# Two thirds of the modulation's product on ScalarE and GpSimd, in a two-block network on one Trainium2 core

## The chip, the cores and the metric

The kernel runs on one core of a Trainium2 chip. The engines are TensorE (PE in the profile; PEld is its weight load), VectorE (DVE), ScalarE (ACT), GpSimd (POOL) and SyncE (SP, which issues most of the DMAs). The metric is the device time of one execution in microseconds. A change below about 0.5% can't be told from none.

## The reference

The input is x, 256 tokens of 1024 channels, in fp32. Two blocks follow each other. The first has mixers and a feed-forward, and a norm at its end:

```python
x = x + concat([y_sc, y_gdn, y_sb]) @ w_mix_out
h = rmsnorm(x, w_norm_ffn)
u = causal_dwconv(h @ w_ffn_up, w_ffn_conv)      # 1024 -> 2 * 2816, 3 taps
gate, val = split(u)
x = x + (silu(gate) * val) @ w_ffn_down
```

The second block is modulated by a vector c of 1024 numbers. Six vectors of 1024 are made of it by one vector-matrix product and used in the norms and the residuals; two kinds of attention and a mixture of 32 experts, of which each token takes 4, are the block's layers:

```python
mod = silu(c) @ w_ada + b_ada                    # 1024 -> 6 * 1024
sh1, sc1, gt1, sh2, sc2, gt2 = split(mod, 6)
h = rms_norm(x, g_pre_mix) * (1 + sc1) + sh1
x = x + gt1 * rms_norm(attention(h) @ w_out, g_post_mix)
h2 = rms_norm(x, g_pre_ffn) * (1 + sc2) + sh2
x = x + gt2 * rms_norm(moe_ffn(h2), g_post_ffn)
```

## The kernel before

The program is one straight sequence: block 1's mixers (0 to 183 us), its feed-forward (183 to 396), the norms between the blocks (396 to 405), block 2's attention (405 to 545), the router, and the experts (565 to the end).

**Weights.** The dense weights and the modulation's come in one stream of slabs, 128x2048 fp32, 1 MB each, in the order `WS`, through the six places of pool A (`NA`). `load_slabs` issues on SyncE's queue the load of slab n once slab n - 6 is read. `ADA_AT` says before which dense slab each of the 24 modulation slabs stands; four (`WX`) are not in the stream but have places of their own in pool `fx`, loaded in turns 2 to 5 of the feed-forward. After the stream pool A takes six of the experts' slabs.

**Units and splits.** Half a dense slab is a unit of weights, 128x1024. A product in full fp32 is made of three fast ones, so each unit is split into a high and a low part (`split`): ScalarE copies the high 12 bits (L388), VectorE subtracts them (L393; in a few places GpSimd does), both into one of four places of pool C, tile `u`. `split_ahead` writes the splits up to four units ahead of the products, so the split of unit u + 4 waits until the products of unit u are done.

**The feed-forward.** Its loop runs 11 turns. In a turn i, `up(2 * i)` and `up(2 * i + 1)` take two units each, 24 products a unit (L433) into a PSUM bank; ScalarE takes the bank out with the first tap (L1040, `fcv`), VectorE adds the two others from the bank (L1043). The gate gets its SiLU on ScalarE (L1048), VectorE multiplies (L1049), and the product is split too: `gh` on ScalarE (L1052), `gl` on VectorE (L1053). From turn 1 on, two `down` units follow (12 products each, lines L467 to L469). The four last `down` units come behind the loop, in `last_products`, the first 128 tokens' products before the others', so that the norm of the first half (`add_norms`) runs beside the products of the second.

**The modulation.** `ada(i)` makes 16 of the 48 chunks of 128 from 8 slabs. [...] All 8 slabs add up in one PSUM bank. Then ScalarE copies the bank (`adar`, L489), four transposes turn it (L493), and VectorE adds the bias into `mod` (L494). `ada(0)` runs in the mixers and at the feed-forward's start. Of `ada(1)`, four slabs run at the end of the turns 7 to 10, three after the first half of the norms and one after the second (L483); of `ada(2)`, all eight run in the attention, two after each of the first four heads' keys, in the generator `projections2`. `shifts` makes from the modulation the router's biases and the residual's scales.

**Order.** Everything is written out by hand; in the mixers and the attention `weave` picks between chains by estimated times. Each engine does its instructions in the order in which they were written. `keep_warm(n)` (L292) writes n products that nobody reads, at seven places, with the counts of `WARM`.

Of the kernel before, what the change touches and what calls it, by code (L numbers as in the profile page):

```python
# [10 lines left out]
F32 = mybir.dt.float32  # L11
# [22 lines left out]
# The pools that hold the experts' first slabs; those of pool O hold only one.  # L34
# [4 lines left out]
F1 = 3  # L39
LAST = 2  # L40
# Products that keep the tensor engine's clock up, by place.
WARM = (4, 6, 9, 1, 2, 9, 12)

# Slots of the experts by rank: the first two are experts 0 and 1, the others come by falling count of tokens.
# [4 lines left out]
# The stream of dense weights: ("s", i), slabs of the products; ("a", i), slabs of the modulation, put before the slab  # L49
# of the products with the number given.  # L50
N_DENSE = 67
ADA_AT = [14] * 3 + [20] * 5 + [38, 41, 44, 47] + [-1] * 4 + [54] * 2 + [55] * 2 + [56] * 2 + [57] * 2
# [3 lines left out]
# Slabs of the modulation that have places of their own.  # L56
WX = [("a", j) for j in range(24) if ADA_AT[j] < 0]
WS_ADA = [(WS + WX).index(("a", j)) for j in range(24)]
# [15 lines left out]
# Those after this are of the first block's mixers only.  # L74
NKEPT = COLS["router"][1]
ROWS, NROWS = packed_at(("dt_bias", 4), ("a_log", 4), ("lam", 256), ("b_router", 32), ("g_sub", 128))
# Constants kept throughout, and those of the first and the second block.
# [6 lines left out]
def constants():  # L84
    """Masks and counters that depend on shapes alone."""
# [29 lines left out]
# Latencies between engines that weave reckons with, of the first and of the second block's chains.  # L115
# [46 lines left out]
def kernel(ctx: ExitStack, tc: tile.TileContext, x_in, cols_in, rows_in, const_in, cona_in, conb_in, rpb_in,  # L162
# [29 lines left out]
    def load_slabs(upto=10 ** 6):  # L192
        """Loads the slabs whose places have been read, in the end some of the first expert's."""
# [14 lines left out]
    # the experts' weights, in the order of their use  # L208
# [1850 lines left out]
```

## Time and profile before

| | us |
|---|---|
| median of 3 runs (1525.47 to 1531.39) | 1526.28 |
| span of the profiled execution | 1522.0 |
| TensorE busy | 1392.0 (91%) |
| VectorE busy | 556.7 (37%) |
| ScalarE busy | 445.6 (29%) |
| GpSimd busy | 91.6 (6%) |

The profile is of one execution of its own, whose only time is the span: from its first to its last instruction 1522.0 us, 4.3 below the median of the timed runs. Busy times are totals over stages that differ: in the experts' 950 us VectorE and ScalarE have little to do, while in the feed-forward VectorE is busy for over 70% of the time. GpSimd's 42 instructions lie almost all ahead of 216 us and between 396 and 424 us. What a stage is bound by is therefore read from its own stretch.

### The profile page before, as it was taken

Reading aid. Unit: us, or ns where it says so; the run is one execution under the profiler, and the core shown is the slowest. Engines: PE = TensorE matmul, PEld = TensorE weight load, DVE = VectorE, ACT = ScalarE, POOL = GpSimd, SP = SyncE. Lnnn points to the kernel's source line nnn. Section 1 sums busy time; section 2 is a strip of 40 time slices with the busy share of each in tenths; the row PEclk is TensorE's granted clock in tenths of the full one; section 3 lists DMA queues with packets and bytes.
Section 4 is the critical chain, followed back from the end, with each engine's and each line's share of the span. In section 5 each row is a group of like instructions: output and inputs, shape, how many; then the busy total and the mean of one; then the engine's idle time right before and its main releaser. Section 6 shows DMA issues by size and latency. Waiting matters only on the chain.

```text
span 1522.0 us, 22645 instructions
## 1 busy us (share of the span) xinstructions
PE 1392.0 (91%) x8951; PEld 749.9 (49%) x8951; DVE 556.7 (37%) x1234; ACT 445.6 (29%) x967; POOL 91.6 (6%) x42
## 2 busy tenths in 40 slices
PE   7999979999899999999999999999999977877774
PEld 6898779998678963333333333333333322322211
DVE  4854687776766752222122122212121101110102
ACT  6554545554645541111111111112121101100111
POOL 2322150000310000000000000000000000000000
PEclk9999999999999999999999999999999998999987
DMA  7322575666666488999999899999999999999994
GB/s 308 119 105 84 222 276 215 263 218 224 202 248 222 171 334 353 420 421 421 390 422 410 356 418 412 420 421 419 421 420 421 420 421 421 420 421 421 421 421 198
DMA packets 71088, 506.74 MB, mean 333 GB/s; under 512 B 8096, under 2 KB 8352, under 8 KB 9952
## 3 DMA queue, kind: packets, MB, share of 16 engines
q1 hardware_dynamic: 70112, 503.50, 82.3%
q10 hardware_dynamic: 864, 1.72, 0.3%
q8 instruction: 73, 1.20, 0.3%
q14 instruction: 39, 0.32, 0.1%
HBM read 504.14 MB, written 1.05 MB: 332 GB/s over the span
## 4 chain that ended last, share of the span: by engine, by line
PE 64%; DMA 27%; DVE 4%; ACT 3%; issue 1%; SPq 0%; POOL 0%; ACTq 0%; DVEq 0%; POOLq 0%
DMA w<-in_we 26%; PE mm L1685 18%; PE mm L433 15%; PE mm L1728 7%; PE acc L1751 3%; PE acc L467 2%; PE acc L468 2%; PE acc L469 2%; PE mm L1643 2%; PE mm L1723 2%; DVE u L393 2%; PE mm L1280 1%; PE mm L810 1%; DMA w<-in_ws 1%; PE mm L1654 1%
## 5 line engine op out<-in xcount | busy, mean ns | idle before, releaser
L1685 PE MATMUL mm<-w,xT 128*64 128x512 f32 (+1 forms) x2432 | 463.6, 631 | 56.5 <-DMA w<-in_we 56.1
L1685 PEld LDWEIGHTS mm<-w,xT 128*64 128x64 f32 (+1 forms) x2432 | 136.3, 129 | 365.8 <-issue 256.1
L1694 DVE TENSOR_SCALAR h<-mm 128x256 f32<-128x256 f32 x58 | 24.6, 425 | 726.6 <-PE mm L1690 726.6
L433 PE MATMUL mm<-hTh,u 128*128 128x256 f32 x1376 | 263.0, 289 | 8.9 <-DVE fcv L1043 7.4
L433 PEld LDWEIGHTS mm<-hTh,u 128*128 128x128 f32 x1376 | 220.4, 194 | 17.8 <-issue 13.7
L433 PE MATMUL mm<-hTl,u 128*128 128x256 f32 x688 | 196.5, 286 | 0.6 <-DVE hTl L422 0.6
L393 DVE TENSOR_TENSOR u<-w,u 128x1024 fp32r<-128x1024 f32 x115 | 160.8, 1404 | 69.2 <-ACT u L388 62.4
L1695 ACT ACTIVATE a<-h 128x256 f32<-128x256 f32 x58 | 24.2, 417 | 519.9 <-DVE h L1694 519.9
L388 ACT ACTIVATE u<-w 128x1024 fp32r<-128x1024 f32 x134 | 140.0, 1057 | 37.7 <-PE acc L469 28.2
L1728 PE MATMUL mm<-w,aT 128*64 128x512 f32 x640 | 141.7, 595 | 5.5 <-ACT aT L1706 5.4
L433 PEld LDWEIGHTS mm<-hTl,u 128*128 128x128 f32 x688 | 133.7, 194 | 1.9 <-DVE hTl L422 0.9
L1728 PEld LDWEIGHTS mm<-w,aT 128*64 128x64 f32 x640 | 44.2, 137 | 90.2 <-issue 78.8
L1733 ACT ACTIVATE y<-mm 128x512 f32<-128x512 f32 x38 | 22.7, 597 | 207.4 <-PE mm L1728 138.5
L1723 PE MATMUL mm<-w,aT 128*32 128x512 f32 x576 | 65.7, 595 | 9.9 <-ACT aT L1706 9.9
L1643 PE MATMUL mm<-x,S 128*32 128x256 f32 (+1 forms) x448 | 56.7, 460 | 2.5 <-DVE S L1630 2.5
L1887 POOL TENSOR_TENSOR fs<-fs,x 128x512 f32<-128x512 f32 x1 | 1.3, 1262 | 958.9 <-ACT fr L300 958.9
L393 POOL TENSOR_TENSOR u<-w,u 128x1024 fp32r<-128x1024 f32 x19 | 46.8, 2467 | 135.2 <-ACT u L388 135.2
L1043 DVE SCALAR_TENSOR_TENSOR fcv<-mm,cols,fcv 128x255 f32<-128x255 f32 x88 | 42.4, 482 | 26.6 <-ACT fcv L1040 25.1
L1661 ACT ACTIVATE xT<-mm,mod,gs 128x64 f32<-128x64 f32 (+1 forms) x152 | 46.6, 386 | 2.1 <-PE mm L1654 1.5
L1663 DVE TENSOR_SCALAR xT<-mm,gs,mod 128x64 f32<-128x64 f32 (+1 forms) x152 | 38.7, 319 | 3.0 <-PE mm L1654 3.0
L1723 PEld LDWEIGHTS mm<-w,aT 128*32 128x32 f32 x576 | 16.7, 109 | 46.8 <-issue 30.9
L1643 PEld LDWEIGHTS mm<-x,S 128*32 128x32 f32 (+1 forms) x448 | 18.6, 119 | 39.6 <-issue 28.3
(553 smaller groups left out, 1479.1 us busy)
## 6 DMA issues: line engine op xcount, KB each, us to landing
w<-in_we SPq DMA_DIRECT2D x384, 1024.0 KB, 19.8
w<-in_ws SPq DMA_DIRECT2D x90, 1024.0 KB, 5.0
nb<-in_rpb SPq DMA_DIRECT2D x4, 512.0 KB, 7.8
x<-in_x SPq DMA_DIRECT2D x2, 512.0 KB, 6.1
w<-in_ws SPq DMA_DIRECT2D x2, 512.0 KB, 7.6
bt<-in_b SPq DMA_DIRECT2D x3, 256.0 KB, 8.5
out<-fs SPq DMA_DIRECT2D x3, 256.0 KB, 2.3
grow<-in_wf ACTq DMA_DIRECT2D x1, 512.0 KB, 4.6
```

Source lines behind the costliest of these rows:

```text
L388: nc.scalar.activation(hi, raw, AF.Copy)
L393: eng.tensor_tensor(lo, raw, hi, op=OP.subtract)
L433: nc.tensor.matmul(b[:, 0:T], w[:, k, :], h[:, k, :], start=(n == 0), stop=(n == 3 * KC - 1))
L467: nc.tensor.matmul(o, th[:, kc, t], wh[:, w], start=first, stop=False)
L1043: nc.vector.scalar_tensor_tensor(t[:, sh:], b[:, :T - sh], w(2 - sh), t[:, sh:], op0=OP.mult, op1=OP.add)
L1643: nc.tensor.matmul(b[p * tb:(p + 1) * tb, 0:n], S[:, c, p * tb:(p + 1) * tb], x[:, c, p * n:(p + 1) * n], start=(c == 0), stop=(c == 1))
L1661: nc.scalar.activation(dst, src, AF.Identity, scale=gs[:, kc:kc + 1], bias=mod[:, 24 + kc:25 + kc])
L1663: nc.vector.tensor_scalar(dst, src, gs[:, kc:kc + 1], mod[:, 24 + kc:25 + kc], op0=OP.mult, op1=OP.add)
L1685: nc.tensor.matmul(b[p * tb:(p + 1) * tb, :], xT[:, k, q * tb:(q + 1) * tb], w1(p * nr + rd, kc // 4)[:, kc % 4, :], start=(kc == 0), stop ...
L1723: nc.tensor.matmul(b[p * tb:(p + 1) * tb, :], aT[:, 0, j, p0 * tb:(p0 + 1) * tb], w2(bi)[:, j, h * 512:(h + 1) * 512], start=(bi == 0), st ...
L1728: nc.tensor.matmul(b[p * tb:(p + 1) * tb, :], aT[:, rd, j, p0 * tb:(p0 + 1) * tb], w2(bi)[:, j, p * 512:(p + 1) * 512], start=(bi == 0 and ...
L1751: nc.tensor.matmul(acc[c][h], lhsT, rhs, start=False, stop=False, skip_group_check=True)
```

## The change

`ada(0)` stays as it is. The 16 slabs of `ada(1)` and `ada(2)` stand in the stream before every other dense slab from 20 to 50, so that all are read in the feed-forward; the places of their own are gone, and pool `fx` holds two sums of 128x2048 instead. At the end of each turn from the first on, `ada_ahead` takes the modulation slabs that stand ahead of the next slab to be split: ScalarE scales the slab by its eight numbers of silu(c), one number per partition, in place (the first of eight into the sum), and GpSimd adds it to the sum. After eight slabs a sum holds for each partition what TensorE has still to add over the partitions. `ada_total`, in the norms between the blocks, does that with four products with a tile of ones; copy, transposes and bias are as before (`ada_end`). The attention has no modulation products any more, and two entries of `WARM` are larger.

```diff
-F1 = 3
-WARM = (4, 6, 9, 1, 2, 9, 12)
+WARM = (8, 9, 9, 1, 2, 9, 12)
-ADA_AT = [14] * 3 + [20] * 5 + [38, 41, 44, 47] + [-1] * 4 + [54] * 2 + [55] * 2 + [56] * 2 + [57] * 2
+ADA_AT = [14] * 3 + [20] * 5 + [20 + 2 * i for i in range(16)]
...
+        def ada_ahead():
+            while state["ada"] < 24 and WS_ADA[state["ada"]] < WS_DENSE[min(state["split"] // 2, N_DENSE - 1)]:
+                i, k = divmod(state["ada"], KC)
+                n = WS_ADA[state["ada"]]
+                state["ada"] += 1
+                if k == 0:
+                    ada_sums[i] = fx.tile([P, SW], F32, name="adas")
+                t, w, c = ada_sums[i], s_slab[n], silc[:, k:k + 1]
+                nc.scalar.activation(w if k else t, w, AF.Copy, scale=c)
+                if k:
+                    nc.gpsimd.tensor_add(t, t, w)
+                slab_read(n)
+
+        def ada_total(i):
+            b = bank()
+            for g in range(4):
+                nc.tensor.matmul(b[32 * g:32 * (g + 1), :], ones[:, 0:32], ada_sums[i][:, g * 512:(g + 1) * 512],
+                                 start=True, stop=True)
+            yield from ada_end(i, b)
...
-                    if 2 <= i < 2 + len(WX):
-                        n = len(WS) + i - 2
-                        s_slab[n] = fx.tile([P, SW], F32, name="w")
-                        nc.sync.dma_start(s_slab[n], ws_in[n])
...
-                    if i == 7:
-                        fill = ada(1)
-                    if i >= 7:
-                        next(fill)
+                    if i >= 1:
+                        ada_ahead()
...
-                for _ in range(F1):
-                    next(fill)
+                totals = [ada_total(1), ada_total(2)]
+                for f in totals:
+                    next(f)
                 keep_warm(WARM[0])
...
-                next(fill)
+                for f in totals:
+                    for _ in f:
+                        pass
                 keep_warm(WARM[1])
...
                     yield from values("vd")
-                    fill = ada(2, psa.tile([P, 512], F32, name="acc00"))
                     for i in range(8):
                         if i == 4:
-                            yield from fill
-                            vs["ada"] = True
                             yield from values("vn")
                         yield from keys(i)
-                        if i < 4:
-                            yield next(fill)
-                            yield next(fill)
```

`ada_ahead` finds three slabs in turn 1, two in the turns 3, 5, 7 and 9, and one in the others; each first slab of a sum (in turns 1 and 5) needs no addition. Lines of the changed kernel have other numbers than before: the split's copy is L385 there, `gh` L1077, the gate's SiLU L1073, the first tap L1065, the split's subtraction L390.

On ScalarE, around the end of turn 3, the rows were

```order
L1048 ACTIVATE fcv_2632<-fcv_2632 128x256
L388 ACTIVATE u<-w 128x1024
L1052 ACTIVATE gh<-fcv_2632 128x256
L388 ACTIVATE u<-w 128x1024 x2
L1040 ACTIVATE fcv_2740<-mm,cols 128x256
L388 ACTIVATE u<-w 128x1024
L1040 ACTIVATE fcv_2772<-mm,cols 128x256
```

and now are

```order
L1073 ACTIVATE fcv_2644<-fcv_2644 128x256
L385 ACTIVATE u<-w 128x1024
L1077 ACTIVATE gh<-fcv_2644 128x256
L385 ACTIVATE u<-w 128x1024
L512 ACTIVATE w<-w,silc 128x2048 x2
L385 ACTIVATE u<-w 128x1024
L1065 ACTIVATE fcv_2760<-mm,cols 128x256
L385 ACTIVATE u<-w 128x1024
L1065 ACTIVATE fcv_2792<-mm,cols 128x256
```

Two scalings of 128x2048 stand between the split copies of the third and the fourth unit of the next turn.

On ScalarE at the end of the loop, where the function table is loaded for the norms, the rows were

```order
L1040 ACTIVATE fcv_3917<-mm,cols 128x256
L1048 ACTIVATE fcv_3883<-fcv_3883 128x256
L1081 ACT_TABLE_LOAD
L388 ACTIVATE u<-w 128x1024
L1052 ACTIVATE gh<-fcv_3883 128x256
L1091 ACTIVATE mm,ss_3972<-xn 128x512
```

and now are

```order
L1065 ACTIVATE fcv_3956<-mm,cols 128x256
L1073 ACTIVATE fcv_3922<-fcv_3922 128x256
L512 ACTIVATE w<-w,silc 128x2048
L1100 ACT_TABLE_LOAD
L385 ACTIVATE u<-w 128x1024
L1077 ACTIVATE gh<-fcv_3922 128x256
L1110 ACTIVATE mm,ss_4003<-xn 128x512
```

The last scaling stands ahead of the last unit's split copy and of the last `gh`. VectorE's order in the feed-forward is the same as before.

On TensorE in the attention, between two heads' keys (L1224 or L1247 are the scores, L1258 or L1281 transposes, L1280 or L1303 the products with the values), the rows were

```order
L433 MATMUL mm<-hTl,u 128x256
L433 MATMUL mm<-hTh,u 128x256
L483 MATMUL acc_4259<-w,silc 32x512 x4
L1258 MATMUL mm<-cst,s 128x128 x8
L483 MATMUL acc_4259<-w,silc 32x512 x4
L1224 MATMUL acc_4571<-k_4489,q_4537 128x256 x2
L1224 MATMUL acc_4572<-k_4489,q_4537 128x256 x2
L1280 MATMUL mm<-vd,e 128x128 x8
```

and now are

```order
L430 MATMUL mm<-hTl,u 128x256
L430 MATMUL mm<-hTh,u 128x256
L1303 MATMUL mm<-vd,e 128x128 x8
L1281 MATMUL mm<-cst,s 128x128 x8
L1247 MATMUL acc_4599<-k_4491,q_4539 128x256 x2
L1247 MATMUL acc_4600<-k_4491,q_4539 128x256 x2
```

The two slabs' products are gone, and the steps of the heads' chains follow each other without them.

## Rows read from the trace of the kernel before

**Rows 1.** Busy us (count) of PE, PEld, DVE, ACT, POOL; PEclk, DMA, GB/s
```profile
300.13:317.25 17.12, 17.12 (x122) 16.02 (x122) 12.42 (x18) 9.14 (x14) 0.00 (x0) 1.00 0.64 246
317.25:335.36 18.11, 18.11 (x129) 15.90 (x128) 12.42 (x18) 10.10 (x15) 0.00 (x0) 1.00 0.57 200
...
437.77:476.48 38.71, 38.71 (x307) 31.60 (x308) 23.32 (x48) 20.41 (x63) 0.00 (x0) 1.00 0.77 283
476.48:545.00 68.52, 68.52 (x473) 61.72 (x472) 44.75 (x92) 37.17 (x89) 0.00 (x0) 1.00 0.57 217
```

**Rows 2.** The same view, ahead of the experts
```profile
556.00:576.00 20.00, 18.26 (x107) 8.38 (x107) 9.17 (x45) 5.99 (x14) 0.00 (x0) 1.00 0.71 266
```

**Rows 3.** The chain that ended last, whole span: start us, us, what
```profile
1083.83 18.16 DMA w<-in_we
```

**Rows 4.** The modulation's products from 376 us on: durations min/median/max ns
```profile
L483 PE MATMUL acc<-w,silc x64: 592/593/616, 433.6 to 469.4; 128*32 128x512 f32 x64
```

**Rows 5.** The chain in the attention
```profile
467.01 0.99 PE acc L483 x8
...
473.30 0.43 PE mm L493 x4
```

**Rows 6.** GpSimd's timeline: start us, us, line, what, [idle before <-releaser]
```profile
200.07 4.09 POOL L1017 TENSOR_TENSOR bt<-bt,b1q 96x2048 f32<-96x2048 f32 x1
...
413.05 10.57 POOL L1163 TENSOR_TENSOR nb<-nb,cb 128x2048 f32<-128x2048 f32 x2 [2.04 <-PE acc L469]
```

**Rows 7.** VectorE's timeline at the same times
```profile
200.78 4.47 DVE L393 TENSOR_TENSOR u<-w,u 128x1024 fp32r<-128x1024 f32 x1 [4.17 <-PE mm L433]
205.18 0.99 DVE L1043 SCALAR_TENSOR_TENSOR fcv<-mm,cols,fcv 128x255 f32<-128x255 f32 x2
...
412.47 12.23 DVE L393 TENSOR_TENSOR u<-w,u 128x1024 fp32r<-128x1024 f32 x3 [0.69 <-ACT u L388]
```

**Rows 8.** VectorE's groups, 231.65 to 317.25 us: busy us, mean ns | idle before
```profile
L393 DVE TENSOR_TENSOR u<-w,u 128x1024 fp32r<-128x1024 f32 x30 | 36.7, 1223 | 9.7 <-ACT u L388 9.6
```

**Rows 9.** ScalarE's groups in the same stretch
```profile
L388 ACT ACTIVATE u<-w 128x1024 fp32r<-128x1024 f32 x30 | 31.6, 1053 | 10.2 <-PE acc L469 10.2
```

**Rows 10.** The chain in the feed-forward: up units of two turns
```profile
231.65 11.51 PE mm L433 x96
...
265.89 11.51 PE mm L433 x96
```

**Rows 11.** ScalarE's timeline in the feed-forward
```profile
228.66 0.42 ACT L1052 ACTIVATE gh<-fcv 128x256 fp32r<-128x256 f32 x1 [0.86 <-DVE fcv L1049]
...
263.11 1.06 ACT L388 ACTIVATE u<-w 128x1024 fp32r<-128x1024 f32 x1 [0.32 <-PE acc L469]
265.92 1.06 ACT L388 ACTIVATE u<-w 128x1024 fp32r<-128x1024 f32 x1 [1.75 <-PE acc L469]
```

**Rows 12.** The chain at the feed-forward's end
```profile
383.71 0.99 PE mm L483 x8
...
389.85 0.70 DVE xn L1090
```

**Rows 13.** Timeline of ScalarE and VectorE at the feed-forward's end
```profile
384.12 0.41 ACT L1048 ACTIVATE fcv<-fcv 128x256 f32<-128x256 f32 x1
...
384.54 1.28 ACT L1081 ACT_TABLE_LOAD   x1
...
388.07 0.42 DVE L1053 TENSOR_TENSOR gl<-fcv,gh 128x256 fp32r<-128x256 f32 x1
```

**Rows 14.** Busy times in five us of the feed-forward's start
```profile
215.00:220.00 5.00, 1.76 (x8) 1.79 (x9) 4.86 (x6) 1.34 (x3) 1.10 (x1) 0.55 0.01 3
```

**Rows 15.** The chain at the same place
```profile
218.24 7.79 PE mm L433 x48
```

**Rows 16.** TensorE's timeline in the norms between the blocks
```profile
403.87 1.48 PE L292 MATMUL mm<-warm 128*128 128x512 bf16 x6
408.64 0.66 PE L493 MATMUL mm<-cst,adar 128*128 128x128 f32 x4 [1.45 <-ACT adar L489]
```

More of the change, by code (lines that the diff above doesn't have):

```diff
@@ L55 @@
 WS_DENSE = [i for i, w in enumerate(WS) if w[0] == "s"]
-WX = [("a", j) for j in range(24) if ADA_AT[j] < 0]
-WS_ADA = [(WS + WX).index(("a", j)) for j in range(24)]
+WS_ADA = [WS.index(("a", j)) for j in range(24)]
 MIX_KC = [6, 7, 0, 1, 2, 3, 4, 5]
@@ L473, in split_into, with ada @@
             (eng or nc.vector).tensor_tensor(lo, src, hi, op=OP.subtract)
-        def ada(i, b=None):
-            b = bank() if b is None else b
+        def ada(i):
+            b = bank()
             for k in range(KC):
@@ L487, in ada, with ada_end @@
                     yield 0.94, 0
+            yield from ada_end(i, b)
+        def ada_end(i, b):
             r = hp.tile([P, 512], F32, name="adar", tag="wide")
@@ L498, in ada @@
             yield 0.3, 0
+        ada_sums = {}
+        def ada_ahead():
[11 more added lines that the diff above has]
+        def ada_total(i):
+            b = bank()
+            for g in range(4):
+                nc.tensor.matmul(b[32 * g:32 * (g + 1), :], ones[:, 0:32], ada_sums[i][:, g * 512:(g + 1) * 512],
+                                 start=True, stop=True)
+            yield from ada_end(i, b)
         with ExitStack() as s1:
@@ L1005 @@
             sf = s2.enter_context(ExitStack())
-            fx = sf.enter_context(tc.tile_pool(name="fx", bufs=len(WX)))
+            fx = sf.enter_context(tc.tile_pool(name="fx", bufs=2))
             with ExitStack() as s3:
@@ L1134 @@
                 flipped(xn[:, 0, :], 0, take_mod)
-                for _ in range(F1):
-                    next(fill)
+                assert state["ada"] == 24
+                totals = [ada_total(1), ada_total(2)]
+                for f in totals:
+                    next(f)
                 keep_warm(WARM[0])
@@ L1327, in shifts @@
                     yield 0, 1.0
-                    yield from fill
-                    yield 0, 4.0
                     b = bank()
@@ L1339, in shifts @@
                         yield 0, 1.5
-                    while "ada" not in vs:
-                        yield 0, 0.1
                     nc.vector.tensor_mul(gg2, mod[:, 40:48], col("g_post_ffn"))
@@ L1351, in projections2 @@
                     yield from values("vd")
-                    fill = ada(2, psa.tile([P, 512], F32, name="acc00"))
                     for i in range(8):
                         if i == 4:
-                            yield from fill
-                            vs["ada"] = True
                             yield from values("vn")
                         yield from keys(i)
-                        if i < 4:
-                            yield next(fill)
-                            yield next(fill)
                     load_all("B")
@@ L2000, in pack @@
     assert len(S["s"]) == N_DENSE
-    ws = np.stack([S[k][i] for k, i in WS + WX], 0)
+    ws = np.stack([S[k][i] for k, i in WS], 0)
     w1, wd = f("w1_2")[0], f("w2_2")[0]
```

## The prediction, made before the changed kernel ran

> **What bounds the kernel now.** I read the busy time by stretches first, then the chain of work that ended last, then the engines' timelines at the places the change touches. In the feed-forward the first thing to see is a stretch in which TensorE has no gap: one turn of its loop (four up units, two down units) takes 17.12 us and TensorE is busy for 17.12 us of it, while VectorE is busy for 12.42 and ScalarE for 9.14 [rows 1]. A turn that also holds one modulation slab takes 18.11 [rows 1]. The attention is the same picture: 38.71 us of 38.71 and 68.52 of 68.52 busy [rows 1]. So in both stages what is taken off TensorE shortens the program, if nothing else becomes late. The experts after that wait in the chain for their weights' transfers only from 1084 us on [rows 3]; between 556 and 576 us the DMA engines have idle time (266 GB/s, 0.71 busy) [rows 2], so the expert slabs that can be loaded ahead are loaded by then, and the rest follow places that TensorE frees. I therefore take it that the end moves by as much as the end of the attention moves.
>
> **What is removed.** A modulation slab costs TensorE 0.99 us (8 products, four in parallel columns) [rows 5]. Sixteen slabs leave it. Four were run inside the feed-forward: 4 x 0.99 = 3.96 us, all on the path (18.11 - 17.12 = 0.99 confirms it) [rows 1]. Four were run in the norms behind it, where TensorE waits for the norm's chain anyway and fills the rest with products nobody reads [rows 16]: 0. Eight were run in the attention (64 products) [rows 4] with one set of transposes, 0.43 us: 8 x 0.99 + 0.43 = 8.35 us on the path [rows 5]. Removed: 12.3 us.
>
> **What is added, and where it waits.** In place of each slab, ScalarE scales 128x2048 in the feed-forward and GpSimd adds it to a sum: 16 scalings and 14 additions (the first of each sum needs none). A scaling is estimated at 2 x 1.05 = 2.1 us from the 128x1024 copy [rows 9]. An addition's price has two near rows: 4.09 us (96x2048, in place) and the pair of 128x2048 in 10.57 us [rows 6]. In that pair the first addition begins when VectorE's first split ends (412.47 + 1.22 = 413.69, 0.64 us in), and one split of 1.22 stands between the two, so one is (10.57 - 0.64 - 1.22) / 2 = 4.4. I take 4.4, the row with the same shape. The Trainium skill (GPSIMD Engine Reference, 3.1 Elementwise) gives 4.5 us for an fp32 addition of 2048; with nine additions on the path below, the sum would be 0.9 us higher by it.
>
> GpSimd is not alone, and this is the main point. While GpSimd's subtraction ran from 200.07 to 204.16, VectorE's split, 1.22 us on its own [rows 8], took 4.47 and ended 1.1 us after it; the convolution steps, which read PSUM and one tile, kept their 0.99 for two beside the next GpSimd instruction [rows 6, 7]. At 412.47 three splits took 12.23 us beside two additions: one split gets in between two additions, no more [rows 7]. So an addition of 4.4 us holds back VectorE's next operation on two SBUF tiles. The Trainium skill (SBUF — State Buffer, Who interferes with whom) has it as an exclusive lock between GpSimd and a VectorE instruction with two SBUF inputs, the loser waiting for the whole instruction; the trace agrees (4.47 for 1.22). By that rule all 14 additions block, not only those that rows here show.
>
> How much of that TensorE sees: the split of the unit four ahead starts when a unit's place is read (265.92 behind the turn's start at 265.89) [rows 10, 11]. A unit takes 11.51 / 4 = 2.88, so the weights are wanted 8.63 us later, and the split takes 1.05 + 1.22: a lead of 6.3 us. One addition (4.4 + 1.22) fits into it; two with a late VectorE don't. Times below count from a turn's start, and a unit wants its low part 0.2 us after it begins.
>
> - **First catch-up** (turn from 231.65). Three scalings stand behind `gh`, which ends at 229.08, -2.57 [rows 10, 11]. They end at -0.47, 1.63 and 3.73, the two splits' copies at 4.78 and 5.83. The first addition runs from 1.63 to 6.03, the third unit's low part is ready at 7.25 and wanted at 5.96: 1.3 late. The second addition runs to 11.65, the fourth's low part is ready at 12.87, wanted at 10.1: 2.8 late. I take 4.0; with 4.09 it is 3.4, and 5 if ScalarE's copies are slower.
> - **Turns with two additions** (two of the middle ones). The first scaling ends at 263.11 + 1.06 + 2.1 = 266.3, 0.4 into the turn that begins at 265.89 [rows 10, 11]; addition, split, addition, split end at 0.4 + 2 x 5.62 = 11.6, wanted at 11.7: no loss if VectorE is on time. It isn't: it has 17.12 - 12.42 = 4.7 us to spare per turn, 32.9 in the seven middle turns, and nine additions cost it 4.4 less the 0.99 that it can do beside each, 3.4, so 30.6. What it is late stays, some 2 us, and `gh` and the scalings stand behind it. I take 2.2 for each: 4.4; ends 0 and 9.
> - **The end of the feed-forward.** Counted from the last up unit's end at 383.71, the first half of the last products is read at 389.85, 6.14 later, or 5.15 without the slab [rows 12]. Now two additions come in this turn: -11.1 to -6.7 and, a split later, -5.5 to -1.1. The first of the last four units' low part is ready at 0.1. Then VectorE does a pair, the gate's product and a split (2.7) and the next pair (3.7), the SiLU follows at 4.1, and ScalarE's sixteenth scaling stands before its table load: 6.2, table 7.5, last copy 8.6 [rows 9, 13]. The last addition, 6.2 to 10.6, holds the last split to 11.8 and `gl` to 12.2; the half is done at 12.5. That is 7.3 later than 5.15, and 9.5 with VectorE 2.2 late. I take 8.0; ends 6 and 10. The norms wait for this half.
> - **Clock.** After the long wait before 218 us the granted clock was 0.55, which is near the lower level, 1.2 GHz, and 48 products took 7.79 us for 5.76 [rows 10, 14, 15]: 2.0 lost. Around the feed-forward's end TensorE is idle for half of some 13 us: half of that, 1.0; ends 0 and 3.
> - **Norms.** Two passes over the sums, 0.99 each by the same form, lie in the time of the removed slabs. The wait of 1.45 for the `adar` copy goes [rows 16], but two such copies now stand before the splits on ScalarE, and seven more unread products before the values' first. 0.5; ends -1.5 and 2.
>
> The slabs' transfers come earlier, 1.5 more per turn. A turn moves 246 GB/s with the DMA engines 0.64 busy [rows 1], so there is room, and I count no term for it: a slab of the sums holds its place until it is added, a few us more than now, and if that cover fails the next dense slab is late by one addition, which the high end contains.
>
> **Sum.** -12.3 + 4.0 + 4.4 + 8.0 + 1.0 + 0.5 = +5.6 us. The profiled execution spans 1522.0, 4.3 below the median of the runs, 1526.28; I add the shift to the median: **1531.9**. All low ends give -4.8 (1521.5); all high ends, with half of the attention's gain lost, +21 (1547).
>
> **Rivals.**
> - *The lead hides the additions.* For it: 6.3 us of lead against 5.6 for one addition; against: the bunches above. Then the two middle terms are 0 and the end costs 3.4 (scaling and table before the last copy): -12.3 + 3.4 + 0.5 = -8.4, **1518**.
> - *VectorE becomes the bound of the feed-forward*, the other side. If it does nothing beside an addition, nine turns need 9 x 12.42 + 14 x 4.4 = 173.4 for 154.1: +19.3 in place of the first two terms, and 6 + 1.5 for end and clock: +14.5, **1541**. It decides from the point where an addition costs VectorE over 4.7 x 9 / 14 = 3.0 us; I reckon 3.4, so it is near.
> - *The attention gives nothing back*, because its heads' chains and not TensorE set it. Against it: the second stretch is without slabs and as full [rows 1]. 8.35 more: **1540**.
> - *The end doesn't follow the attention's end*, since the weights' stream sets it: **1526**. Against it: the idle DMA before the experts [rows 2].
>
> **Chances.** Forecast 0.50 (its own range 1526 to 1538), hidden 0.17, VectorE the bound 0.18, attention 0.10, stream 0.05. A measurement here can tell about 0.5%, 7.6 us, from no change. Faster by more than that: 0.12, most of the first rival. Within it: 0.33 of the forecast, 0.05 of the first and the last rival each: 0.43. Slower: 0.17 of the forecast and the second and third rivals: 0.45. The range goes from the first rival to beyond the second: 1518 to 1545.
>
> **What would show it.** Right: splits on VectorE of 4 to 6 us wherever a GpSimd addition runs; TensorE idle on the low parts at about 237 to 244 us, in the turns with two additions and by several us before the norms; the attention 8 us shorter. Wrong: turns of 17.12 throughout the feed-forward with additions in them (first rival), turns of 19 (second), or new TensorE waits in the attention (third).

## The result, and the profile after

The changed kernel is slower: 1543.25 us, median of 4 runs (1542.60 to 1543.78), against 1525.88 for the kernel before on the same chip; the ratio is 1.0109 (95% interval 1.0094 to 1.0125). The profiled execution spans 1542.0 us where the one before spanned 1522.0. The forecast was 1531.9, +5.6; the medians are 17.4 apart, the profiles 20.0.

The 20 us can be laid out by marks that both traces have: the second copy `gh` of a turn on ScalarE (L1052 before, L1077 now), VectorE's reading of the first half of the feed-forward's result (L1090, now L1109), the first key's product behind the values (L433, now L430) and the first unread product behind the attention. Busy us by engine between these marks, first the kernel before, in the columns of [rows 1]:

```profile
228.66:367.50 138.84, 138.84 (x975) 127.97 (x974) 99.38 (x145) 73.02 (x112) 0.00 (x0) 1.00 0.62 228
367.50:389.85 22.35, 22.35 (x149) 18.61 (x149) 14.02 (x21) 10.84 (x16) 0.00 (x0) 1.00 0.68 243
389.85:424.84 34.99, 30.04 (x153) 20.55 (x152) 30.33 (x48) 19.93 (x46) 19.03 (x5) 0.95 0.61 186
424.84:549.23 124.39, 122.61 (x874) 104.15 (x872) 76.91 (x154) 65.37 (x166) 0.00 (x0) 1.00 0.65 243
```

and the changed kernel, with two single turns of the loop at the end:

```profile
228.20:382.39 154.19, 143.89 (x974) 131.97 (x973) 128.79 (x145) 95.42 (x126) 53.43 (x11) 0.99 0.67 253
382.39:410.31 27.92, 18.87 (x120) 16.08 (x119) 23.08 (x22) 16.18 (x19) 14.84 (x3) 0.93 0.55 205
410.31:454.49 44.18, 33.88 (x150) 23.59 (x151) 32.14 (x52) 21.17 (x48) 17.39 (x5) 0.89 0.59 186
454.49:568.94 114.45, 113.33 (x803) 101.97 (x802) 74.58 (x150) 63.81 (x163) 0.00 (x0) 1.00 0.50 186
...
252.28:269.88 17.60, 17.37 (x122) 16.07 (x121) 15.70 (x19) 10.82 (x15) 4.63 (x1) 1.00 0.65 238
269.88:290.98 21.10, 18.48 (x129) 16.90 (x128) 17.24 (x19) 12.59 (x17) 10.10 (x2) 1.00 0.58 223
```

| stage | before | after | difference | forecast |
|---|---|---|---|---|
| eight turns of the feed-forward | 138.84 | 154.19 | +15.4 | +6.4 |
| its end, to the first half's reading | 22.35 | 27.92 | +5.6 | +7.0 |
| norms and values | 34.99 | 44.18 | +9.2 | +0.5 |
| heads and output projection | 124.39 | 114.45 | -9.9 | -8.35 |
| ahead of and behind all this | 1201.4 | 1201.3 | -0.2 | 0 |

(The forecast's column has two of the four slabs that left the feed-forward in the turns and two in its end, and the 1.0 for the clock in the end.)

The border between the first two stages is a mark on ScalarE, and ScalarE and VectorE run ahead of TensorE. At the first mark they lead it by some 3 us (`gh` at 228.20, TensorE's next turn from 231.18). In the kernel before they keep this lead; now it is gone after one turn (252.28 and 252.21) and doesn't come back (382.39 and 382.60). So 3 us of the eight turns' 15.4 are lead used up, and TensorE pays for them only at the end. Counted from TensorE's first up product of a turn, the eight turns take 140.4 us before (231.49 to 371.93) and 151.4 now (231.18 to 382.60), and from there to the first half's reading it is 17.9 and 27.7: +11.0 and +9.8. By these marks, with three of the four slabs in the turns, the forecast had +5.4 and +8.0. TensorE's rows in the first turn, up to the start of the next:

```profile
231.18 0.28 PE L430 MATMUL mm<-hTh,u 128*128 128x256 f32 x1
...
238.35 0.51 PE L430 MATMUL mm<-hTh,u 128*128 128x256 f32 x2 [1.03 <-DVE u L390]
...
243.86 0.51 PE L430 MATMUL mm<-hTh,u 128*128 128x256 f32 x2 [2.38 <-DVE u L390]
...
252.21 0.28 PE L430 MATMUL mm<-hTh,u 128*128 128x256 f32 x1
```

TensorE, full before in these eight turns and in the end, is now busy for 143.9 of 154.2 us in the turns. What it waits for between 226 and 412 us (engine, line, releaser: us in total, times, longest):

```profile
PE acc L465 <- DVE u L390: 11.7, 6, 2.9
PE mm L430 <- DVE u L390: 5.4, 7, 2.4
PE acc L464 <- ACT gh L1077: 2.2, 1, 2.2
```

It is the splits' low parts: at the up units (L430) most of all in the first turn, 3.4 of the 5.4; at the down units (L465) 2.4 in each of the two turns with two additions, and 6.9 at the end. VectorE's timeline has these splits in the first turn, in one with one addition and in one with two; [rows 8] had 1.22 for each:

```profile
235.28 8.52 DVE L390 TENSOR_TENSOR u<-w,u 128x1024 fp32r<-128x1024 f32 x2 [5.65 <-ACT u L385]
...
256.53 4.88 DVE L390 TENSOR_TENSOR u<-w,u 128x1024 fp32r<-128x1024 f32 x1 [1.55 <-ACT u L385]
...
276.02 3.00 DVE L390 TENSOR_TENSOR u<-w,u 128x1024 fp32r<-128x1024 f32 x1 [3.51 <-ACT u L385]
...
279.84 4.71 DVE L390 TENSOR_TENSOR u<-w,u 128x1024 fp32r<-128x1024 f32 x1
```

GpSimd's timeline has the additions beside them:

```profile
232.55 10.17 POOL L514 TENSOR_TENSOR adas<-adas,w 128x2048 f32<-128x2048 f32 x2 [16.90 <-ACT w L512]
255.69 4.63 POOL L514 TENSOR_TENSOR adas<-adas,w 128x2048 f32<-128x2048 f32 x1 [12.97 <-ACT w L512]
273.29 10.18 POOL L514 TENSOR_TENSOR adas<-adas,w 128x2048 f32<-128x2048 f32 x2 [12.96 <-ACT w L512]
```

and ScalarE's what stands ahead of the second of these places:

```profile
253.56 1.99 ACT L512 ACTIVATE w<-w,silc 128x2048 f32<-128x2048 f32 x1
255.45 1.04 ACT L385 ACTIVATE u<-w 128x1024 fp32r<-128x1024 f32 x1
```

The end of a scaling (255.55) lets two things start at once: the addition on GpSimd (255.69) and the next split copy on ScalarE (255.45). So behind one scaling the split comes to VectorE (256.53) 0.8 us into the addition and waits for the rest of it. Behind two scalings it comes 2.7 us into the first addition (276.02 beside 273.29). And before that, VectorE stood idle behind the scalings, 1.55 us here and 3.51 there.

**An account of VectorE's time** follows. A turn is longer than 17.12 by what GpSimd holds, plus the idle time before the held split, less the 4.7 us that VectorE had to spare (17.12 - 12.42 [rows 1]):

- one addition: 4.88 - 1.22 + 1.55 - 4.7 = 0.5; the turn takes 17.60, 0.48 longer;
- two: 3.00 + 4.71 - 2.44 + 3.51 - 4.7 = 4.1; 21.10, 3.98 longer;
- the first turn: 8.52 - 2.44 + 5.65 - 4.7 = 7.0; 24.08, 6.96 longer, of which TensorE lost 3.9 in the turn itself.

This is bookkeeping with each turn's own rows: it closes because VectorE has hardly any other idle time in these turns. It says where the time went; whether it can forecast a turn is another question.

### The profile page after: what moved, and what is told of

Same layout as the page of the kernel before. It is cut to its first block, busy times and chain, and to the rows that moved or that the text cites. A ratio compares the mean times of both kernels' runs of the same rounds, so it can differ in the third digit from the quotient of the medians.

```text
span 1542.0 us, 22466 instructions
## 1 busy us (share of the span) xinstructions
PE 1385.6 (90%) x8842; PEld 751.5 (49%) x8846; DVE 591.7 (38%) x1234; ACT 472.8 (31%) x983; POOL 158.2 (10%) x56
## 4 chain that ended last, share of the span: by engine, by line
PE 52%; DMA 27%; DVE 12%; ACT 6%; issue 3%; SPq 0%; POOL 0%; ACTq 0%; DVEq 0%; POOLq 0%
DMA w<-in_we 26%; PE mm L1698 18%; PE mm L430 7%; DVE u L390 7%; PE mm L1741 6%; PE acc L1764 3%; PE mm L1656 2%; PE mm L1736 2%; DVE fcv L1068 2%; ACT u L385 2%; DMA w<-in_ws 1%; PE acc L465 1%; PE acc L466 1%; PE acc L464 1%; ACT w L512 1%
## 5 line engine op out<-in xcount | busy, mean ns | idle before, releaser
L430 PE MATMUL mm<-hTh,u 128*128 128x256 f32 x1376 | 265.0, 290 | 14.0 <-DVE u L390 5.9
L430 PEld LDWEIGHTS mm<-hTh,u 128*128 128x128 f32 x1376 | 220.5, 194 | 23.0 <-issue 8.8
L390 DVE TENSOR_TENSOR u<-w,u 128x1024 fp32r<-128x1024 f32 x115 | 187.4, 1635 | 76.9 <-ACT u L385 76.9
L430 PE MATMUL mm<-hTl,u 128*128 128x256 f32 x688 | 196.5, 286 | 0.6 <-DVE hTl L419 0.6
L385 ACT ACTIVATE u<-w 128x1024 fp32r<-128x1024 f32 x134 | 139.4, 1053 | 20.0 <-PE acc L466 9.1
L430 PEld LDWEIGHTS mm<-hTl,u 128*128 128x128 f32 x688 | 133.6, 194 | 2.1 <-DVE hTl L419 0.9
L514 POOL TENSOR_TENSOR adas<-adas,w 128x2048 f32<-128x2048 f32 x14 | 68.3, 4877 | 123.9 <-ACT w L512 123.6
L390 POOL TENSOR_TENSOR u<-w,u 128x1024 fp32r<-128x1024 f32 x19 | 46.7, 2459 | 140.1 <-ACT u L385 140.1
L465 PE MATMUL acc<-u,gh 128*128 128x512 f32 x88 | 36.9, 420 | 11.7 <-DVE u L390 11.7
L1676 DVE TENSOR_SCALAR xT<-mm,gs,mod 128x64 f32<-128x64 f32 (+1 forms) x152 | 38.7, 320 | 3.0 <-PE mm L1667 3.0
```

The source lines that it names most:

```text
L385: nc.scalar.activation(hi, raw, AF.Copy)
L390: eng.tensor_tensor(lo, raw, hi, op=OP.subtract)
L430: nc.tensor.matmul(b[:, 0:T], w[:, k, :], h[:, k, :], start=(n == 0), stop=(n == 3 * KC - 1))
L465: nc.tensor.matmul(o, th[:, kc, t], wl[:, w], start=False, stop=False)
L514: nc.gpsimd.tensor_add(t, t, w)
```

## Experiments

The table has the stages by the same marks (feed-forward: from the first mark to the first half's reading), and the timed runs. Behind the attention the profiled executions took 970.6 to 975.4 us, with nothing changed there, so small effects are read from the stages. The ratio is to the kernel before as timed beside each run; its median there was 1524.2 to 1525.9 us.

| kernel | feed-forward | norms, values | heads | median us | ratio to before |
|---|---|---|---|---|---|
| before | 161.2 | 35.0 | 124.4 | 1525.88 | |
| changed | 182.1 | 44.2 | 114.5 | 1543.25 | 1.0109 (1.0094 to 1.0125) |
| e1 no additions | 158.7 | 43.4 | 114.5 | 1521.46 | 0.9983 (0.9973 to 0.9993) |
| e2 additions on VectorE | 160.2 | 43.1 | 114.5 | 1522.12 | 0.9982 (0.9970 to 0.9993) |
| e3 four pieces | 163.2 | 43.8 | 114.5 | 1525.87 | 1.0002 (0.9992 to 1.0012) |
| e4 fused on VectorE | 158.4 | 41.8 | 114.5 | 1519.84 | 0.9966 (0.9956 to 0.9975) |
| e5 spread | 189.4 | 43.1 | 114.4 | 1553.62 | 1.0177 (1.0159 to 1.0195) |
| e6 e4, two tiles | 158.5 | 38.7 | 114.5 | 1518.38 | 0.9947 (0.9931 to 0.9962) |
| e7 e4, fewer unread | 158.5 | 41.8 | 114.5 | 1518.84 | 0.9945 (0.9929 to 0.9961) |
| e8 all four | 157.0 | 38.9 | 114.5 | 1516.38 | 0.9929 (0.9911 to 0.9947) |
| e9 unscaled additions | 172.8 | 43.4 | 114.5 | 1534.73 | 1.0072 (1.0057 to 1.0087) |
| e10 changed, two tiles | 182.1 | 42.8 | 114.5 | 1544.38 | 1.0129 (1.0113 to 1.0144) |
| e11 e8, bias later | 157.2 | 34.3 | 115.4 | 1512.68 | 0.9926 (0.9912 to 0.9939) |
| e12 changed, two tiles, bias later | 182.1 | 35.3 | 115.4 | 1538.13 | 1.0090 (1.0073 to 1.0107) |
| e13 before, bias later | 161.3 | 31.1 | 125.3 | 1521.72 | 0.9982 (0.9970 to 0.9993) |

### Additions or scalings: e1 to e4

```diff
-                if k:
-                    nc.gpsimd.tensor_add(t, t, w)
```

> The changed kernel with its 14 GpSimd additions left out (the sums hold their first slab only); the 16 scalings on ScalarE stay where they are. Between the end of the last product's gate copy in turn 1 and the reading of the first half of the feed-forward's result the changed kernel needs 182.1 us where the kernel before needed 161.2. Theory 1 (the additions hold VectorE's splits): a scaling's end starts the addition on GpSimd and the next split copy on ScalarE together, so the split reaches VectorE some 0.8 us into an addition and waits for all of it. Then the turns with one and with two scalings fall back to 17.1 to 17.3 us, the first catch-up turn to under 18, what is left is the last scaling and the table load at the end (3 to 4 us) and the norms: 1521 us (1517 to 1526). Theory 2 (the scalings themselves, 2 us each ahead of the split copies on ScalarE, make the low parts late): the two-scaling turns stay near 20 and the first near 22; 1536 us (1531 to 1543).

1521.46: theory 1. The two-scaling turn from 261.38 takes 17.13, although VectorE waits in it behind two scalings:

```profile
267.95 1.23 DVE L390 TENSOR_TENSOR u<-w,u 128x1024 fp32r<-128x1024 f32 x1 [3.51 <-ACT u L385]
```

That idle time fits into the 4.7. So a wait behind scalings costs nothing by itself; it costs when a hold comes on top.

```diff
-                    nc.gpsimd.tensor_add(t, t, w)
+                    nc.vector.tensor_add(t, t, w)
```

> The changed kernel with the 14 additions on VectorE in place of GpSimd; the scalings stay. An addition of 128x2048 by VectorE should take twice the 1.22 us of a 128x1024 split, so 14 x 2.4 = 34 us more of VectorE's time. Theory 1 (GpSimd's hold): VectorE has 4.7 us to spare in a turn, so one addition fits and two just do; 1524 us (1519 to 1530). Theory 2 (scalings on ScalarE): 1537 us (1531 to 1543). Theory 3 (the feed-forward is simply bound by VectorE's total work, whoever holds it up): the turns with two additions come to 12.4 + 4.8 = 17.2 us and nothing is lost but in the first and at the end, so the time can't tell 1 from 3, but single-addition turns of 17.1 with VectorE busy for 14.9 would.

1522.12, again theory 1: the same work, in the same places, and some 20 us less. The group of additions on VectorE in this kernel (busy us, mean ns | idle before):

```profile
L514 DVE TENSOR_TENSOR adas<-adas,w 128x2048 f32<-128x2048 f32 x14 | 32.1, 2292 | 8.6 <-ACT w L512 8.2
```

2.29 us is all that an addition takes from VectorE here, where a lone one on GpSimd took 3.66 by holding it, and two together 5.27.

```diff
-                    nc.gpsimd.tensor_add(t, t, w)
+                    for g in range(4):
+                        o = slice(g * 512, (g + 1) * 512)
+                        nc.gpsimd.tensor_add(t[:, o], t[:, o], w[:, o])
```

> The changed kernel with each GpSimd addition cut into four of 128x512, one after the other; the same work, the same place. Theory 1: a split has to wait for the piece that runs, about 1.2 us, not for all 4.6, and VectorE comes in between pieces: the turns with two additions fall from 21.1 to under 18.5; 1529 us (1522 to 1535). Rival (what counts is GpSimd's whole time, since a split that waits is overtaken by the next piece, or the last piece's end is late): 1543 us, within 4. Theory 2 (scalings): 1541 us (1537 to 1545).

1525.87: the hold lasts as long as the one instruction that runs. GpSimd needs longer for the four pieces, up to 7.22 us instead of 4.63, and the splits beside them 1.4 to 2.3 instead of 4.7:

```profile
254.17 7.22 POOL L516 TENSOR_TENSOR adas<-adas,w 128x512 f32<-128x512 f32 x4 [6.29 <-ACT w L512]
...
275.45 1.41 DVE L390 TENSOR_TENSOR u<-w,u 128x1024 fp32r<-128x1024 f32 x1
...
278.23 2.32 DVE L390 TENSOR_TENSOR u<-w,u 128x1024 fp32r<-128x1024 f32 x1
```

The fourth edit puts scaling and addition into one instruction of VectorE:

```diff
-                nc.scalar.activation(w if k else t, w, AF.Copy, scale=c)
                 if k:
-                    nc.gpsimd.tensor_add(t, t, w)
+                    nc.vector.scalar_tensor_tensor(t, w, c, t, op0=OP.mult, op1=OP.add)
+                else:
+                    nc.vector.tensor_scalar(t, w, c, None, op0=OP.mult)
```

> Each slab scaled and added by one VectorE instruction (multiply by the column, add the sum; the first of a sum a scaling alone), ScalarE's 16 scalings and GpSimd's 14 additions gone. VectorE's instruction should take about 2.4 us if it costs as much per element as the split. Theory 1 and theory 2 both: the feed-forward's middle turns at 17.1 us; one instruction of 2.4 at its end; 1519 us (1514 to 1525). The difference to the run with the additions alone moved is what the scalings cost by themselves: 1 to 4 us by theory 1, over 10 by theory 2. If VectorE in fact has no room (theory 3), the turns with two instructions come to 18 and more and the time is 1526 or above.

1519.84, as expected. 2.35 us for each instruction, nearly as much as the addition alone; against e2 the scalings are gone and 2.3 us, within theory 1's 1 to 4 (the ratios' intervals just overlap).

### The account put to the test: e5 and e9

```diff
-ADA_AT = [14] * 3 + [20] * 5 + [20 + 2 * i for i in range(16)]
+ADA_AT = [14] * 3 + [20] * 5 + [24 + 3 * i // 2 for i in range(16)]
...
                     up(2 * i)
+                    if i >= 2:
+                        ada_ahead()
```

> The changed kernel, GpSimd's additions kept, but the 16 slabs stand in the weights' stream before dense slabs 24, 25, 27, 28, ... 46 and are scaled and added one per half turn (the call stands after the first up pair too), so that no two additions follow each other and none is in the last two turns. Theory 1, with the rule that one addition fits into the lead of 6.3 us and a bunch doesn't: an addition by itself costs what it does in the single-addition turns of the changed kernel, 0.47 us, so 14 x 0.47 = 6.6 us in place of 17.3 in the turns, and the end is as in the kernel before without its slab, 7 us less: 1526 us (1521 to 1531). Rival, VectorE's total time is the bound: two additions a turn of 4.6 us each, of which 0.99 can be done beside, make 12.4 + 7.2 = 19.6 us a turn for 17.1, seven turns of +2.5, so 17.5 us in place of 17.3 and only the end is won: 1536 us (1532 to 1540).

1553.62, ten slower than the changed kernel: both expectations fell. The turn from 249.14 takes 22.09 us. Its two splits beside additions:

```profile
253.38 4.89 DVE L390 TENSOR_TENSOR u<-w,u 128x1024 fp32r<-128x1024 f32 x1 [1.55 <-ACT u L385]
...
262.57 4.81 DVE L390 TENSOR_TENSOR u<-w,u 128x1024 fp32r<-128x1024 f32 x1 [0.82 <-ACT u L385]
```

With these rows the account gives 4.89 + 4.81 - 2.44 + 1.55 + 0.82 - 4.7 = 4.9 for it; measured 4.97. That closes the books of this turn, but forecasts nothing. Six turns take 22.1 to 22.5 here, and the spare time of the last ones, which have no addition, is of no use to them; in the changed kernel five of the seven middle turns have a single addition, which their 4.7 us nearly cover. That one addition "costs 0.47 us" was the remainder of a budget, and not a price that adds up.

```diff
-                nc.scalar.activation(w if k else t, w, AF.Copy, scale=c)
-                if k:
+                if not k:
+                    nc.scalar.activation(t, w, AF.Copy, scale=c)
+                else:
                     nc.gpsimd.tensor_add(t, t, w)
```

> The changed kernel with its 14 additions on GpSimd, but the scalings of the added slabs left out (the slabs are added as loaded; the first slab of each sum is still scaled). An account of VectorE's time fits the turns seen so far: a turn is longer by what GpSimd holds VectorE's splits (3.66 us for one addition, 5.27 for two together) plus the time that VectorE waits for a split copy that stands behind scalings on ScalarE (1.55 behind one, 3.51 behind two, 5.65 behind three), less the 4.7 us that it has to spare. By this account the hold alone is 14 x 3.66 = 51 us for 9 x 4.7 = 42 us to spare, so the turns lose 5 to 9 us in place of 17.3 and the end some 3 less: 1530 us (1525 to 1534). Rival (the hold alone makes the loss, the wait behind the scalings lies beside it): 1541 us (1537 to 1545).

1534.73, 0.7 above the account's range and 2 below the rival's: the only time that the account forecast, and it was somewhat low. It had taken the additions to stay in their turns. They now start when a slab lands: four fall into the first turn, which takes 28.9 us (227.69 to 256.62 by `gh`), and they hold other steps too, the gate's product (L1075) and `gl` (L1079), 0.42 each otherwise:

```profile
247.94 3.69 DVE L1075 TENSOR_TENSOR fcv<-fcv,fcv 128x256 f32<-128x256 f32 x1
...
270.36 4.38 DVE L1079 TENSOR_TENSOR gl<-fcv,gh 128x256 fp32r<-128x256 f32 x1
```

### The norms: e6 to e8 and e10 to e13

The norms lose 8 us even in e1, without an addition, so this is a cost of its own. In the changed kernel the timelines of ScalarE, of VectorE and of GpSimd show two suspects there:

```profile
428.21 0.60 ACT L489 ACTIVATE adar<-mm 128x512 f32<-128x512 f32 x1 [3.15 <-PE mm L493]
...
428.71 1.99 ACT L385 ACTIVATE u<-w 128x1024 fp32r<-128x1024 f32 x2
430.60 2.89 ACT L1143 ACTIVATE hm<-mm,mod,gm 128x128 f32<-128x128 f32 x8
```

```profile
436.43 4.46 DVE L1192 SCALAR_TENSOR_TENSOR lamt<-rows 128x64 f32<-128x64 f32 x1
...
441.17 4.17 DVE L1196 SCALAR_TENSOR_TENSOR lam<-lam 128x1 f32<-128x1 f32 x1 [0.27 <-ACT lam L1195]
...
445.36 3.48 DVE L390 TENSOR_TENSOR u<-w,u 128x1024 fp32r<-128x1024 f32 x3
```

```profile
436.22 9.10 POOL L1186 TENSOR_TENSOR nb<-nb,cb 128x2048 f32<-128x2048 f32 x2
```

Both sums' rows go through one tile `adar`, so the second copy waits 3.15 us for the first row's transposes, with two split copies and the second half's modulation (`hm`) behind it. And the grid's bias (L1186, in [rows 6] as L1163) now starts ahead of two tiny steps, which it holds for 4.46 and 4.17 us, and the values' three splits come behind those; in the kernel before the first split was 0.6 us ahead of it [rows 6, 7].

```diff
-            r = hp.tile([P, 512], F32, name="adar", tag="wide")
+            r = (fx.tile([P, 512], F32, name="adar") if i else hp.tile([P, 512], F32, name="adar", tag="wide"))
```

> The version with one VectorE instruction per slab, and each sum's row copied from PSUM into a tile of its own (they shared one, so that ScalarE waited 1.48 us with the second copy for the transposes of the first, ahead of two split copies and of the second half's modulation). Theory A (this shared tile is what the norms lost): the second half's first modulation comes 1.5 us earlier and the attention with it: 1.5 us less than the version with the shared tile, some 1518 us. Theory B (what the norms lost is the unread products, which now wait for a PSUM bank that the modulation frees, and hold TensorE ahead of the transposes and of the values' first product): no difference, within 0.5 us.

Theory A: norms 38.7 for 41.8, twice what was expected. The medians are 1.5 apart, but they were timed beside different runs of the kernel before, and the ratios' intervals overlap.

```diff
-WARM = (8, 9, 9, 1, 2, 9, 12)
+WARM = (4, 6, 9, 1, 2, 9, 12)
```

> The version with one VectorE instruction per slab (shared tile kept), with 4 and 6 unread products in the norms, as in the kernel before, in place of 8 and 9. Theory A (shared tile): ScalarE's second copy follows the transposes, which follow four unread products less, 4 x 0.24 = 1 us earlier; 1 us less. Theory B: 1 us before the transposes and 3 x 0.36 = 1.1 before the first value product: 2 us less, some 1518 us. Against both: with fewer products the granted clock falls lower in the values' products and the time is the same or longer (1519 to 1522).

Norms 41.8 as in e4: in the stage the unread products cost nothing. The median, 1518.84, is what theory B had; the ratio's interval overlaps e4's, and no stage up to the end of the attention shows a gain.

e8 takes e4, e6, e7 and e5's places together:

> One VectorE instruction per slab, one per half turn and none in the last two turns, a tile for each sum's row, and 4 and 6 unread products: all that the runs so far point to. From 1519.8: the end of the feed-forward without a slab 2 to 3 us less, the first catch-up turn 0.8 less, the norms 1.5 to 3.5 less: 1514 us (1511 to 1518). If two instructions of 2.35 in one turn are too much for VectorE (12.4 + 4.7 = 17.1), the turns lose up to 0.5 each and the time is 1517.

1516.38: the middle turns take 17.12 each, the feed-forward 157.0, which is the 161.2 before less four slabs (3.96), with 14 additions inside.

> The changed kernel with a tile of its own for each sum's row and nothing else: ScalarE waited 3.15 us with the second copy for the transposes of the first row, ahead of two split copies and the second half's modulation. Theory A: this wait is a third of what the norms lost (44.2 us from the reading of the first half to the values' last product, 35.0 before): 3 us less, 1540 us (1538.5 to 1541.5). Theory B (the values' end is set by GpSimd's addition of the grid's bias and the splits it holds, which comes when it comes): 1543 us, within 1.

Theory B: the stage falls by 1.3 only and the time not at all. In e6 there were 3.1 to win. Here the two tiny steps are through, but the splits come 0.8 us behind the start of the bias addition (GpSimd's row, then VectorE's):

```profile
435.60 10.08 POOL L1186 TENSOR_TENSOR nb<-nb,cb 128x2048 f32<-128x2048 f32 x2 [1.37 <-issue]
```

```profile
436.39 11.51 DVE L390 TENSOR_TENSOR u<-w,u 128x1024 fp32r<-128x1024 f32 x3
```

That is tested by doing the bias on VectorE in the attention:

```diff
...
-                    nc.gpsimd.tensor_tensor(vw, vw, conb("win")[:, None, :].to_broadcast([P, 32, 64]), op=OP.add)
...
                         yield from keys(i)
+                        if i in (1, 2):
+                            vw = nb[:, i - 1].rearrange("p r h c -> p (r h) c")
+                            nc.vector.tensor_tensor(vw, vw, conb("win")[:, None, :].to_broadcast([P, 32, 64]), op=OP.add)
+                            yield [("v", 2.3), ("n", 0)]
```

> The version with all four mends, and the addition of the grid's bias (two of 128x2048, on GpSimd, 9.1 us in which VectorE's splits for the values wait; the kernel before has them too) done by VectorE in the attention, after the second and the third head's keys. If a GpSimd addition costs there what it does in the feed-forward, the values' splits come through, and from the reading of the first half to the first key's product it takes 33 us instead of 39, with 2 x 2.3 us more for VectorE in a stage where it is busy 60%: 1511 us (1508 to 1514). Rival (TensorE at the lower clock, or the heads' chains, take the place): 1515.5 us (1514 to 1518).

1512.68, the fastest kernel here, inside the first range. Its norms are 4.6 shorter than e8's, but its ratio doesn't stand apart from e8's.

> The changed kernel with two edits in the norms and none in the feed-forward: a tile of its own for each sum's row, and the grid's bias added by VectorE in the attention, after the second and the third head's keys, in place of GpSimd at the start of the values. From the reading of the first half to the first key's product the changed kernel takes 44.2 us, the kernel before 35.0. Theory A (what the norms lost is the shared tile, and the bias addition, which now meets two small steps and then all the values' splits, where before the first split was just ahead of it): 35 to 37 us there, 1535.5 us (1533 to 1538). Theory B (it is the rest: ScalarE's copies, PSUM banks, the clock after the long wait): 40 to 41, 1540 us (1538 to 1543).

The stage is theory A's, 35.3 of 44.2. The time, 1538.13, is on the border of both ranges; in the profile the heads take 1.0 and the experts 2.1 more than in the changed kernel. From e10 to e12 the stage falls by 7.6.

> The kernel before with the grid's bias added by VectorE in the attention, after the second and the third head's keys, and nothing else: it tells what GpSimd's addition cost there already. If GpSimd's 10.6 us hold up the values' splits as the feed-forward's additions do, the way from the reading of the first half to the first key's product (35.0) shortens by one to two holds, 3.7 to 5: 1522 us (1520 to 1523.5). Rival (the first split is ahead of it and TensorE has work until the others): 1526 us, within 1.5.

1521.72: the hold was there in the kernel before, 3.9 us of its norms and some 3 of its time.

## Why the prediction was right and wrong

The profile's +20.0 is 14.4 more than the forecast. The turns between the first and the last were 6.1 longer than it had, the end 2.8, and the norms, without the clock's 1.2, 7.5; the heads gave 1.6 more. These and small rests make the difference.

**Removed: right, and a little more.** The heads gave 9.9 for 8.35. TensorE's busy time there fell by 9.28; 0.9 more than the slabs is a pair of row products that now stands ahead of the mark, in the norms, and 0.7 is idle time that went (1.78 to 1.12). The end followed the attention's end, as assumed, within 0.3.

**An addition holds a split: right.** Thirteen of the 14 hold one: 4.8 to 4.9 us for a split that comes behind one scaling, 3.0 behind two, 4.7 beside the second addition of a pair. The last addition holds a small step ahead of the last split (`gm`). An addition took 4.6, not 4.4. The rule of the Trainium skill (SBUF — State Buffer, Who interferes with whom), an exclusive lock for the whole instruction, agrees with all 14, and its advice to put an elementwise sum on VectorE (GPSIMD Engine Reference, 4.1 Engine selection) with e2, where 2.29 us take the place of a hold of 3.66 us.

**First catch-up turn, 4.0: right.** TensorE's turn takes 21.03 us for 17.11 before, 3.9 more. It waits 1.0 us for the third up unit's low part and 2.4 for the fourth's, at 238.35 and 243.86, where the working had them 1.3 and 2.8 late, and for nothing at the down units. By ScalarE's marks the turn is 7.0 longer; the other 3.0 are the lead over TensorE, which the working didn't follow into the next turns.

**Turns after it, 2.2 for each with two additions and nothing for the others: wrong, 4.0 and 0.5.** The failing step is "nine additions cost it 4.4 less the 0.99 that it can do beside each, 3.4, so 30.6". The nine holds come to 26.9 us, less than that. Left out is the time that VectorE stands idle behind the scalings: 1.6 us in each of four turns and 3.51 in each of the three with two scalings, 16.9 in all. Together that is 43.8 us for the 32.9 that it had to spare, 10.9 too much; the seven turns are 10.3 longer (10.5 by TensorE's marks), where the forecast had 4.4. The working had the scalings on ScalarE in front of the split copies, but priced only the additions on VectorE. e1 shows that the idle time alone costs these turns next to nothing, and e9 that the holds alone cost less than the two together (feed-forward 172.8 for 182.1).

With that, an addition in these turns costs 4.9 us of VectorE's time, above the 3.0 that the second rival named as the point from which it decides. So the second rival is what happened here: VectorE sets the pace. Its clue said turns of 19 us; the eight turns' mean by ScalarE's marks is 19.3, though none takes 19: they take 17.5 to 17.6, 21.1 and, once, 24.1. With the end and the clock it had +22.8 for the whole feed-forward; measured are 20.9 and 1.2. That its total, 1541, came near is partly chance: it has nothing for the norms, 8.0 too little without the clock, its heads gave 1.6 too little, and the profiles are 2.6 further apart than the medians.

**End, 8.0: too small, 10.8. The clock, 1.0: right, 1.2.** From the last up unit's end (383.71, now 394.33) to the first half's reading it was to take 5.15 us without the slab; it takes 15.98, and the forecast's ends were 6 and 10. The last addition was to start 6.2 behind that mark with VectorE on time; it starts at 403.10, 8.8 behind it, because the lead was used up: that turn's first mark, `gh` at 382.39, is 11.9 us ahead of the last up unit's end, where it was 15.2 without the slab. With VectorE 2.2 late the working itself had 9.5, and took 8.0. Ahead of the last split stands `gm`, which takes the hold in its place (VectorE's row, GpSimd's, and TensorE's last wait):

```profile
403.38 4.47 DVE L1124 SCALAR_TENSOR_TENSOR gm<-mod,cols 128x8 f32<-128x8 f32 x1
```

```profile
403.10 4.73 POOL L514 TENSOR_TENSOR adas<-adas,w 128x2048 f32<-128x2048 f32 x1 [7.12 <-ACT w L512]
```

```profile
409.05 0.80 PE L465 MATMUL acc<-u,gh 128*128 128x512 f32 x1 [2.86 <-DVE u L390]
```

The clock's 1.2 lie between the two halves' readings. TensorE had stood for 2.2 us on `gh` and 2.9 on a split; then ten products took 4.20 us at a granted clock of 0.50, the lower level of 1.2 GHz, for some 0.23 each at full clock (windows of the changed kernel, in the columns of [rows 1]):

```profile
409.05:413.25 4.20, 4.20 (x10) 3.38 (x11) 3.01 (x6) 2.13 (x6) 0.00 (x0) 0.50 0.85 337
413.25:417.36 4.11, 4.11 (x19) 3.32 (x18) 2.00 (x9) 1.17 (x5) 0.96 (x1) 0.98 0.36 150
```

**Norms, 0.5: wrong, 9.2.** The working saw the copies and the unread products. It didn't follow what stands behind them: of the 9.2, 1.2 is the clock, 0.9 the pair of row products, 1.3 the shared tile (e10; it is 3.1 in e6) and 3.7 the bias addition, which costs 7.6 here (e10 to e12) and 3.9 before (e13). The remaining 2 are open; no run tests them.

**Sums.** Two slips change no conclusion: the low ends as given add up to -4.4, not -4.8, and the second rival's sum leaves the norms' 0.5 out.

## What to carry to other kernels

Work given to an idle GpSimd is paid for by VectorE: price it at the whole instruction, for whatever step with two inputs in SBUF comes next, however small, plus the time that VectorE waits for the engine that feeds both; then set that against VectorE's spare time, turn by turn. Where one event releases GpSimd's instruction and, through ScalarE, VectorE's next step, they overlap each time. Where such an instruction must stay, short pieces can cost far less (e3), and the same sum on VectorE least (e4). And choose the marks of a stage on the engine whose time counts: here marks on ScalarE put 3 us of the end into the first turn.

## What the runs showed of the hardware that was not expected

- A held step needn't be large: 128x8 took 4.47 us beside an addition (`gm`, L1124; 0.16 before), 128x1 took 4.17.
- On VectorE a multiply-add of 128x2048 with a column takes 2.35 us, the addition alone 2.29, and a scaling alone 1.28 (L515 in e4).
- Four GpSimd additions of 128x512 beside a busy VectorE take 6.1 to 7.2 us (e3), one of 128x2048 takes 4.6 (changed kernel).
